# One decoder trunk, four edits: addresses of moving operands, filler pairs, embedding products, a bias table

## The chip, the cores and the metric

The kernel runs on one core of a Trainium2 chip. Its time is the device time of one execution in microseconds (us). Per core there are TensorE (PE in the rows, PEld for its weight loads), VectorE (DVE), ScalarE (ACT), GpSimd (POOL) and SyncE (SP), which issues the DMAs. [...]

## What is computed

The reference is a two-layer decoder over 1,024 tokens of width 1,024, all in float32:

```
h = rms_norm(x, g)
layer 0:  x += rms_norm((gb * conv3(gc * u)) @ w_sc_out)            gb, gc, u = h @ w_sc_in
layer 1:  x += rms_norm(diff_attention(h, k, v, dist_bias) @ w_o)   k, v from x after layer 0
both:     x += rms_norm((silu(gate) * up) @ w_down)                 gate, up = conv3(h @ w_up), 2 x 2816
both:     x += rms_norm(sigmoid(h @ w_gate) * (p_i @ w_proj))       p_i is 1024 x 256
dist_bias = rel_bias[rel_bucket(0..1023)]                           32 buckets x 8 heads
```

conv3 is causal, three taps, per channel.

## The kernel before

**Products.** Every float32 product is made of three `fp32r` matmuls: each operand is cut into a high part (ACT copy) and a low part (DVE subtract), by `split` (L305, L306) for activations and by `wsplit` (L201, L202) or `wcut` (L207, L208) for weights, and high x high, low x high and high x low are summed in PSUM (`mm3`, L318 to L320). The weights, 128 x 128, are stationary; the activations are the moving operand, channels on the partitions and 512 tokens (a "half") or 256 along the row.

**Order.** The program is a list of steps, each with a weight tile (512 KB) that is loaded two steps ahead and cut one step ahead. After each step a few "ticks" advance background generators: `gen_post` (residual, norm, operands of the next part), `gen_up` (operands of the channel mixer). A scheduler that simulates the engines then orders the instructions of each engine by readiness and by the place at which they were written, so an instruction can be issued well before its step.

**Stages.** (1) `sc_mix(0)`, `sc_mix(1)`: for each half 24 steps (moving tiles `hy`), then 8 output steps over the products `z` (moving tiles `s` of the scope `sc`). (2) `ffn(0)`: first `proj_ahead`, the embedding products `p @ w_proj` of both halves (4 steps, 96 matmuls) whose results go to DRAM (`pscr`); then the channel mixer up, NF = 22 pairs of a gate and an up tile. The first NS = 5 pairs are computed for half 0 alone in the plain way (`std_step`, 2 x 48 matmuls of 256 columns, L787); the other 17 for both halves at once by a Winograd scheme with 7 instead of 8 products (`pair_step(f, True)`, 84 matmuls of 512 columns, L809 to L811); the NS first ones are then made up for half 1 (`pair_step(f, False)`, 84 matmuls of 256). The Winograd steps need the sums T1 to T4 of the operands of both halves, which `gen_up` makes on ACT and DVE (L592, L614 to L617, L306); the plain ones need those of half 0 only. (3) `setup_attn` (L1157 to L1183): lambda, and the bias table, by three matmuls with a one-hot matrix (L1176; each float32 one is recorded as two), stores to `gscr` and eight DMAs that spread it over 128 rows of `grep`. Its small tiles come from tag `c2`, 3 buffers, that the convolutions use too. (4) `down`: 44 steps; `jit` loads the mixer's result from `hscr` and cuts it (L924 to L926). (5) `ple(0, half)`: 8 gate steps for each half; `load_pj` reads the embedding products back from `pscr`. (6) attention of layer 1, with its K, Q and V products (`pd`, L318 to L320 and L1114) between the heads' small matmuls. (7) `mix1_out`, `ffn(1)` with its own `proj_ahead`, `down`, `ple(1, half)`, and the end.

**Where tiles lie.** A pool lays its tags out in the order of their first use, each tile rounded up to 32 bytes; the pools follow each other: `cpool` (constants), `wpool` (weights), `work`, `hypool` (40 tiles `hy` of 2,048 bytes), and then the scopes `sc`, `up`, `pq`, `att`, which take turns on the rest. `cpool` begins at a multiple of 64 bytes and holds `cst` (1,572 bytes), `ident` (512), `halo` (416), `gsub` and `neg_lam` (4 each). From these sizes all `hy` tiles and, in `up`, `pq` and `att`, all moving tiles begin at a multiple of 64 bytes, and the weight tiles `wh`, `wl` at 32 past one. In `sc` the tag `u` has three tiles of (512 + 2) x 4 = 2,056 bytes, 2,080 each when rounded up; 3 x 2,080 is 32 past a multiple of 64, so the 24 tiles `s` behind them, which hold `z`, begin at 32 past 64.

Of the kernel before, what the change touches and what calls it, by code (L numbers as in the profile page):

```python
# [15 lines left out]
D = 1024  # L16
S = 1024
HT = 512
ND = 8
NF = 22  # L20
NH = 8
# [17 lines left out]
LAG_A = 2  # L39
LAG_B = 2  # L40
TS = 20
NS = 5
PF = 8
QT = 256
END_P = ((0, 1, 2, 3), (0, 1, 2, 3))
# [18 lines left out]
def _program(tc, nc, a, ctx):  # L64
# [12 lines left out]
    def nm(s):  # L77
        uid[0] += 1
        return f"{s}_{uid[0]}"
# [54 lines left out]
    def grab(dt=F32):  # L134
        al = hy if hy.room(1) else scopes["up"][2]
        return own(al, al(dt))

    def drop(t):
        owner.pop(id(t))[0].free(1)


    cst = cpool.tile([P, C_ALL], F32, tag="cst", name="cst")
    nc.sync.dma_start(out=cst, in_=a["cvec"])
    ident = cpool.tile([P, P], F32, tag="ident", name="ident")
    make_identity(nc, ident)
    halo = cpool.tile([P, 52, 2], F32, tag="halo", name="halo")
    gsub = cpool.tile([P, 1], F32, tag="gsub", name="gsub")
    nc.vector.tensor_scalar(gsub, cst[:, C_SUB:C_SUB + 1], 1.0 - LAM0, None, ALU.mult)
# [75 lines left out]
    def step(fn, w=None, pre=None, need=(), ticks=2, g=None, makes=None):  # L224
        sink[-1].append(dict(fn=fn, w=w, pre=pre, need=need, ticks=ticks, g=g, makes=makes))

    def collect(f, *args):
        sink.append([])
        f(*args)
        return sink.pop()  # L230
# [402 lines left out]
    def drop_ops():  # L633
        for name in ("B11", "B21", "B22", "T1", "T2", "T3", "T4"):
            for hi, lo in ops[name]:
                drop(hi)
                drop(lo)
        ops.clear()
# [9 lines left out]
        ys.append(y)  # L648

    def su():  # L650
        return cur[0].tile([P, HT + 2], F32, tag="u", name=nm("u"), bufs=3)

    def sc_():
        if "up" in scopes:
# [1 line left out]
        return cur[0].tile([P, HT], F32, tag="c", name=nm("c"), bufs=3)  # L656

    def u2():
        return scopes["up"][1].tile([P, 2, HT + 2], F32, tag="u2", name=nm("u2"), bufs=2)

    def c2(dt=F32):
        return scopes["up"][1].tile([P, 2, HT], dt, tag="c2", name=nm("c2"), bufs=3)
# [105 lines left out]
    def ffn(L, filler):  # L768
# [3 lines left out]
        def std_step(f, up, hold):  # L772

            def fn(w):
                n = f + NF * up
                p_ = ps()
                for tb in range(2):
                    o = p_[:, tb * QT:(tb + 1) * QT]
                    for k in range(ND):
                        if k >= 4:  # L780
                            hi, lo = (t[:, 0:QT] for t in ops["B22" if tb else "B21"][k - 4])
                        elif tb:
                            hi, lo = ops["F"][k][:, 0:QT], ops["F"][k][:, QT:]
                        else:
                            hi, lo = (t[:, 0:QT] for t in ops["B11"][k])
                        for i, (x, y) in enumerate(((w[0], hi), (w[1], hi), (w[0], lo))):
                            last_mm[0] = nc.tensor.matmul(o, x[:, k128(k)], y, skip_group_check=True,  # L787
                                                          start=(tb == 0 and k == 0 and i == 0),
                                                          stop=(k == ND - 1 and i == 2)).ins
                u = u2()[:, 0, :]  # L790
                nc.scalar.copy(out=u[:, 2:], in_=p_)
                c = conv(p_, u, 8 + n, 0, C_FF + 3 * (44 * L + n), p_)
                if not up:
                    nc.scalar.activation(c, c, AF.Silu)
                    hold["g"] = c
                else:
                    nc.vector.tensor_tensor(c, hold["g"], c, ALU.mult)
                    store(0, f, c)
                    if f == NS - 1:
                        for t in ops["F"]:  # L800
                            drop(t)
            return fn
# [19 lines left out]
        def pair_step(f, both):  # L822

            def fn(w):
                cols = slice(0, HT) if both else slice(QT, HT)
                m = HT if both else QT
                hs = slice(0, 2) if both else slice(1, 2)
                n1, n2 = f, f + NF
                wc1, wc2 = (C_FF + 3 * (44 * L + n) for n in (n1, n2))

                def v(t):
                    return t[:, 0:m].rearrange("p (h c) -> p h c", c=QT)

                def keep(p_):
                    t = wk("rb", bufs=3)
                    nc.scalar.copy(out=t[:, 0:m], in_=p_[:, 0:m])
                    return t

                a_, b_, c_ = ps(), ps(), ps()
                u, g = u2(), u2()  # L840
                product(a_[:, 0:m], w["A11"], "B11", cols, True, True)
                p1 = keep(a_)
                product(b_[:, 0:m], w["A12"], "B21", cols, True, True)
                nc.vector.tensor_tensor(g[:, hs, 2:2 + QT], v(b_), v(p1), ALU.add)
                product(a_[:, 0:m], w["S2"], "T2", cols, False, True)
                q2 = keep(a_)
                product(c_[:, 0:m], w["S1"], "T1", cols, True, True)
                p5 = keep(c_)
                product(a_[:, 0:m], w["S3"], "T3", cols, False, True)
                nc.vector.tensor_tensor(u[:, hs, 2 + QT:], v(a_), v(p5), ALU.add)  # L850
                product(c_[:, 0:m], w["S4"], "B22", cols, False, True)
                nc.vector.tensor_tensor(g[:, hs, 2 + QT:], v(c_), v(q2), ALU.add)
                if both:
                    cg = conv_both(g, wc1)
                else:
                    cg = conv(None, g[:, 1, :], 8 + n1, 1, wc1, g[:, 1, 2:])
                nc.scalar.activation(cg, cg, AF.Silu)
                product(a_[:, 0:m], w["A22"], "T4", cols, False, True)
                nc.scalar.copy(out=u[:, hs, 2:2 + QT], in_=v(a_))
                if both:  # L860
                    cu = conv_both(u, wc2)
                else:
                    cu = conv(None, u[:, 1, :], 8 + n2, 1, wc2, u[:, 1, 2:])
                nc.vector.tensor_tensor(cu, cg, cu, ALU.mult)
                if both:
                    for half in range(2):
                        store(half, f, cu[:, half, :])
                else:
                    store(1, f, cu)
            return fn  # L870

        def wup(n):
            return a["w_ffn_up"][L, n]

        steps.extend(filler)
        for f in range(NS):
            hold = {}
            for up in range(2):
                step(std_step(f, up, hold), wup(f + NF * up), need=[("h0", L)], ticks=4)
        for f in range(NS, NF):  # L880
            step(pair_step(f, True), (wup(f), wup(f + NF)), need=[("T", L)])
        for f in range(NS):
            step(pair_step(f, False), (wup(f), wup(f + NF)))
        step(lambda _: drop_ops(), None, ticks=0)
        if L == 0:
            step(lambda _: setup_attn(), None, ticks=0)
        order = [(half, k) for half in range(2) for g in range(2) for k in range(NF)]
        ahead = deque()
        at = [0]

        def fetch():
            while at[0] < len(order) and len(ahead) < PF:
                half, k = order[at[0]]
                at[0] += 1
                t = scopes["up"][2]()
                nc.sync.dma_start(out=t, in_=hscr[half, k])
                ahead.append(t)

        def jit():
            fetch()  # L900
            t = ahead.popleft()
            j = c2(F32R)
            split(j[:, 0, :], j[:, 1, :], t)
            scopes["up"][2].free(1)
            return j

        def down(half):
# [36 lines left out]

    def ple(L, half, targets):
        pj = []
        def load_pj(_):
            for n in range(ND):
                t = sc_alloc("pq")()()
                nc.sync.dma_start(out=t, in_=pscr[half, n])  # L950
                pj.append(t)

        step(load_pj, None, ticks=0)
        ys = []
        acc = [None]
        key = (f"ple{L}", half)
# [1 line left out]
        def gate_step(n):  # L958
            def fn(w):
# [13 lines left out]
                ys.append(y)  # L973
                if n == ND - 1:
                    free_h(key)
                    scopes["pq"][2].free(ND)
                    have[f"y_ple{L}", half] = (ys, acc[0])
                    bg.append(gen_post(half, (f"y_ple{L}", half), f"post_ple{L}", targets, last=(L == 1),
                                       spill=(L == 0), defer=(L == 0)))
# [389 lines left out]
    bg.append(gen_first(0))  # L1369
    step(lambda _: bg.append(gen_first(1)), None, need=[("mix0", 0)], ticks=0)  # L1370
    sc_mix(0)
    sc_mix(1)
    step(close_scope("sc"), None, ticks=0)
    step(open_scope("up", TS), None, ticks=0)
    for L in range(2):
        ffn(L, collect(proj_ahead, L, 0) + collect(proj_ahead, L, 1))
        step(close_scope("up"), None, ticks=0)
        step(open_scope("pq", 28), None, ticks=0)
        if L == 0:
# [105 lines left out]
```

## Time and profile before

| | us |
|---|---|
| median of the runs (2741.11, 2741.92, 4281.74) | 2741.92 |
| the profiled execution's own time | 2739.69 |
| its span, first to last instruction | 2737.9 |
| TensorE busy | 2587.8 |
| VectorE busy | 1854.8 |
| ScalarE busy | 1286.3 |
| mean granted clock of TensorE | 0.974 |

The profiled execution lies 2.2 us below the median and 1.8 us above its span. In the rows, busy time of TensorE counts a matmul to its modelled end; as matmuls overlap, the distance between two starts tells the rate. "[6.02 <-ACT wh L207]" behind an instruction is the idle time of its engine before it, and what ended it.

### The profile page before, as it was taken

To read this page: it belongs to the slowest core of one execution; us is meant where nothing else is said; L and a number is where in the kernel's file an instruction comes from. 1 tells how busy PE (TensorE), PEld (TensorE's weight loads), DVE (VectorE), ACT (ScalarE), POOL (GpSimd) and SP (SyncE) were. 2 spreads that over 40 slices of the span, in tenths; PEclk is the share of its full clock that TensorE was granted. 3 is DMA by queue.
4 is the path that set the end of the run, shared out by engine and by line. 5 is a ranking of instruction groups with operands and counts; after the bars stand their busy time and mean duration, and the time that the engine had idled before them with its cause. 6 is when DMAs were issued, how large, how long until landed. Compare 5 with 4: busy or idle time off the path is not lost.

```text
span 2737.9 us, 35057 instructions
## 1 busy us (share of the span) xinstructions
PE 2587.8 (95%) x12958; PEld 2127.0 (78%) x12958; DVE 1854.8 (68%) x3166; ACT 1286.3 (47%) x2182; POOL 109.4 (4%) x318
## 2 busy tenths in 40 slices
PE   8999998999997999996999999899799999899995
PEld 7888887888885887875788878688688888787875
DVE  7546469777786458569566665558886768647667
ACT  5233355444444445446555555446444445444542
POOL 0000002000000000000000000000000000000001
PEclk9999999999998999997999999999899999999997
DMA  5233252222225664343111111266222222656342
GB/s 179 93 100 123 92 186 97 85 77 85 77 93 195 231 213 154 123 142 120 55 47 55 47 62 47 93 223 217 77 70 85 77 85 97 238 189 207 116 169 77
DMA packets 128571, 328.39 MB, mean 120 GB/s; under 512 B 14360, under 2 KB 16704, under 8 KB 128400
## 3 DMA queue, kind: packets, MB, share of 16 engines
q1 hardware_dynamic: 128400, 326.16, 34.9%
q8 instruction: 101, 1.65, 0.3%
q14 instruction: 70, 0.57, 0.1%
HBM read 270.49 MB, written 60.33 MB: 121 GB/s over the span
## 4 chain that ended last, share of the span: by engine, by line
PE 87%; DVE 6%; ACT 3%; DMA 2%; issue 2%; DVEq 0%; SPq 0%; ACTq 0%
PE ps L809 8%; PE ps L810 8%; PE ps L811 8%; PE ps L318 8%; PE ps L319 8%; PE ps L320 8%; PE ps L926 6%; PE ps L924 6%; PE ps L925 6%; PE ps L787 4%; PE pd L1114 4%; PE qk L1221 3%; PE pd L318 2%; PE st L1262 2%; PE pd L319 2%; PE pd L320 2%
## 5 line engine op out<-in xcount | busy, mean ns | idle before, releaser
L202 DVE TENSOR_TENSOR wl<-wr,wh 128x1024 fp32r<-128x1024 f32 x228 | 278.9, 1224 | 237.9 <-ACT wh L201 189.4
L201 ACT CAST wh<-wr 128x1024 fp32r<-128x1024 f32 x228 | 239.6, 1053 | 337.9 <-PE ps L926 151.4
L809 PE MATMUL ps<-hy,wh 128*128 128x512 f32 (+1 forms) x924 | 337.8, 374 | 17.0 <-ACT hy L305 11.0
L810 PE MATMUL ps<-hy,wl 128*128 128x512 f32 (+1 forms) x924 | 344.2, 374 | 10.2 <-DVE wl L208 10.2
L924 PE MATMUL ps<-c,wh 128*128 128x512 f32 x704 | 281.8, 400 | 5.2 <-ACT c L305 5.2
L925 PE MATMUL ps<-c,wl 128*128 128x512 f32 x704 | 281.0, 399 | 0.0
L207 ACT CAST wh<-wr 128x1024 fp32r<-128x1024 f32 x132 | 138.3, 1050 | 214.4 <-PE ps L811 191.5
L926 PE MATMUL ps<-c,wh 128*128 128x512 f32 x704 | 232.1, 398 | 2.0 <-DVE c L306 2.0
L811 PE MATMUL ps<-hy,wh 128*128 128x512 f32 (+1 forms) x616 | 229.2, 373 | 4.6 <-DVE hy L306 4.6
L318 PE MATMUL ps<-hy,wh 128*128 128x512 f32 x552 | 220.4, 400 | 7.2 <-ACT hy L390 7.2
L319 PE MATMUL ps<-hy,wl 128*128 128x512 f32 x552 | 219.8, 399 | 0.0
L320 PE MATMUL ps<-hy,wh 128*128 128x512 f32 x552 | 219.2, 398 | 0.0
L809 PEld LDWEIGHTS ps<-hy,wh 128*128 128x128 f32 x924 | 173.8, 190 | 51.9 <-ACT hy L305 12.4
L810 PEld LDWEIGHTS ps<-hy,wl 128*128 128x128 f32 x924 | 175.7, 190 | 45.3 <-DVE wl L208 12.5
L208 DVE TENSOR_TENSOR wl<-wr,wh 128x1024 fp32r<-128x1024 f32 x132 | 161.0, 1223 | 22.0 <-ACT wh L207 21.7
L924 PEld LDWEIGHTS ps<-c,wh 128*128 128x128 f32 x704 | 133.8, 190 | 38.1 <-ACT c L305 5.9
L811 PE MATMUL ps<-s,wh 128*128 128x512 f32 (+1 forms) x440 | 162.1, 370 | 0.0
L926 PEld LDWEIGHTS ps<-c,wh 128*128 128x128 f32 x704 | 132.9, 189 | 35.4 <-DVE c L306 3.7
L925 PEld LDWEIGHTS ps<-c,wl 128*128 128x128 f32 x704 | 133.9, 190 | 32.1
L305 ACT CAST c<-s 128x512 fp32r<-128x512 f32 x176 | 108.6, 619 | 102.6 <-PE ps L926 94.2
L331 DVE TENSOR_TENSOR acc<-acc,sq 128x512 f32<-128x512 f32 x165 | 112.9, 688 | 60.7 <-ACT sq L330 58.2
L306 DVE TENSOR_TENSOR c<-s,c 128x512 fp32r<-128x512 f32 x176 | 120.8, 688 | 47.5 <-ACT c L305 47.5
(233 smaller groups left out, 5669.8 us busy)
## 6 DMA issues: line engine op xcount, KB each, us to landing
wr<-w_ffn_up SPq DMA_DIRECT2D x108, 512.0 KB, 3.4
s<-hscr SPq DMA_DIRECT2D x176, 256.0 KB, 3.4
wr<-w_ffn_down SPq DMA_DIRECT2D x88, 512.0 KB, 3.3
wr<-w_sc_in SPq DMA_DIRECT2D x48, 512.0 KB, 3.3
hscr<-c SPq DMA_DIRECT2D x88, 256.0 KB, 3.1
wr<-w_ple_gate SPq DMA_DIRECT2D x32, 512.0 KB, 3.3
xscr<-hy SPq DMA_DIRECT2D x40, 256.0 KB, 2.4
hy<-xscr SPq DMA_DIRECT2D x40, 256.0 KB, 5.5
```

What stands on the lines that cost most here:

```text
L201: nc.scalar.copy(out=hi[:, :n], in_=raw[:, :n])
L202: nc.vector.tensor_tensor(lo[:, :n], raw[:, :n], hi[:, :n].bitcast(F32), ALU.subtract)
L208: nc.vector.tensor_tensor(lo, src, hi.bitcast(F32), ALU.subtract)
L318: nc.tensor.matmul(out, whi[:, c], hi, start=(i == 0), stop=False)
L319: nc.tensor.matmul(out, wlo[:, c], hi, start=False, stop=False)
L320: last_mm[0] = nc.tensor.matmul(out, whi[:, c], lo, start=False, stop=(i == n - 1)).ins
L809: nc.tensor.matmul(o, hi[:, c], bh, skip_group_check=True, start=start and j == 0, stop=False)
L810: nc.tensor.matmul(o, lo[:, c], bh, skip_group_check=True, start=False, stop=False)
L811: last_mm[0] = nc.tensor.matmul(o, hi[:, c], bl, skip_group_check=True, start=False, stop=stop and j == 3).ins
L924: nc.tensor.matmul(o, hi[:, c], j[:, 0, :], start=(k == 0), stop=False)
L925: nc.tensor.matmul(o, lo[:, c], j[:, 0, :], start=False, stop=False)
L926: last_mm[0] = nc.tensor.matmul(o, hi[:, c], j[:, 1, :], start=False, stop=(k == NF - 1)).ins
```

## The change

1. Two unused tiles of 32 bytes in `cpool` (`pad0` before `ident`, `pad1` behind it) and one in `work` (`pad`); `u` and `u2` rows are 528 floats instead of 514. By the sizes above, `hy`, `ident` and the tiles `s`, `c2`, `kq`, `w5h`, `w5l` of all scopes then begin at 32 past 64, the weights stay at 32 past 64, and attention's `s` and `at`, stationary operands, go from 32 to 0.
2. NS is 8 in layer 0 and 7 in layer 1.
3. Layer 0's embedding products leave the start of `ffn(0)`: each half's two steps stand ahead of its gate steps in `ple(0, half)`, and their results stay in `pq` tiles. Layer 1 is as before.
4. `setup_attn` stands between `sc_mix(0)` and `sc_mix(1)`, with tiles `c` of `sc` (3 buffers).
5. `fetch` is called once before the last make-up step and may take `hy` tiles.

```diff
+UW = 528
-NS = 5
+NS = (8, 7)
...
+    def grab_up(dt=F32):
+        al = scopes["up"][2] if scopes["up"][2].room(1) else hy
+        return own(al, al(dt))
...
+    cpool.tile([P, 8], F32, tag="pad0", name="pad0")
+    work.tile([P, 8], F32, tag="pad", name="pad", bufs=1)
     ident = cpool.tile([P, P], F32, tag="ident", name="ident")
     make_identity(nc, ident)
+    cpool.tile([P, 8], F32, tag="pad1", name="pad1")
...
     def su():
-        return cur[0].tile([P, HT + 2], F32, tag="u", name=nm("u"), bufs=3)
+        return cur[0].tile([P, UW], F32, tag="u", name=nm("u"), bufs=3)[:, 0:HT + 2]
...
     def u2():
-        return scopes["up"][1].tile([P, 2, HT + 2], F32, tag="u2", name=nm("u2"), bufs=2)
+        return scopes["up"][1].tile([P, 2, UW], F32, tag="u2", name=nm("u2"), bufs=2)[:, :, 0:HT + 2]
...
-        for f in range(NS):
+        for f in range(NS[L]):
             hold = {}
             for up in range(2):
                 step(std_step(f, up, hold), wup(f + NF * up), need=[("h0", L)], ticks=4)
-        for f in range(NS, NF):
+        for f in range(NS[L], NF):
             step(pair_step(f, True), (wup(f), wup(f + NF)), need=[("T", L)])
-        for f in range(NS):
+        for f in range(NS[L]):
             step(pair_step(f, False), (wup(f), wup(f + NF)))
+            if f == NS[L] - 2:
+                step(lambda _: fetch(), None, ticks=0)
         step(lambda _: drop_ops(), None, ticks=0)
-        if L == 0:
-            step(lambda _: setup_attn(), None, ticks=0)
+        def fetch():
+            while at[0] < len(order) and len(ahead) < PF:
+                half, k = order[at[0]]
+                if not can(1):
+                    break
+                at[0] += 1
+                t = grab_up()
+                nc.sync.dma_start(out=t, in_=hscr[half, k])
+                ahead.append(t)
...
     def ple(L, half, targets):
         pj = []
+        pt = []
+
+        def load_p():
+            for k in range(2):
+                t = wk("hn")
+                nc.sync.dma_start(out=t, in_=a["pT"][L, half, k])
+                hi, lo = sc_alloc("pq")()(F32R), sc_alloc("pq")()(F32R)
+                split(hi, lo, t)
+                pt.append((hi, lo))
+
+        def proj_step(b):
+            def fn(w):
+                if b == 0:
+                    load_p()
+                for n in range(4):
+                    p_ = ps()
+                    mm3(p_, w[0], w[1], pt, lambda i: slice((n * 2 + i) * P, (n * 2 + i + 1) * P))
+                    t = sc_alloc("pq")()()
+                    nc.scalar.copy(out=t, in_=p_)
+                    pj.append(t)
+            return fn
...
-        step(load_pj, None, ticks=0)
+        if L == 0:
+            for b in range(2):
+                step(proj_step(b), a["w_ple_proj"][L, b])
+        else:
+            step(load_pj, None, ticks=0)
...
     sc_mix(0)
+    step(lambda _: setup_attn(), None, ticks=0)
     sc_mix(1)
...
-        ffn(L, collect(proj_ahead, L, 0) + collect(proj_ahead, L, 1))
+        ffn(L, collect(proj_ahead, 1, 0) + collect(proj_ahead, 1, 1) if L else [])
```

## Rows read from the trace of the kernel before

**Rows 1.** The page: the chain that ended last, share of the span by engine.

```profile
PE 87%; DVE 6%; ACT 3%; DMA 2%; issue 2%; DVEq 0%; SPq 0%; ACTq 0%
```

**Rows 2.** Windows: stretch, length, busy us (count) by engine, granted clock, DMA share, GB/s.

```profile
147.00:190.00 43.00, 43.00 (x191) 35.61 (x190) 17.47 (x20) 16.77 (x25) 0.18 (x1) 1.00 0.32 102
500.00:543.00 43.00, 43.00 (x186) 34.68 (x185) 34.01 (x38) 19.23 (x25) 1.23 (x9) 1.00 0.23 76
...
2420.00:2463.00 43.00, 43.00 (x185) 34.60 (x185) 20.76 (x25) 17.47 (x25) 0.00 (x0) 1.00 0.56 188
```

**Rows 3.** Timeline of TensorE: first matmul over `z` of half 0, first after the last.

```profile
146.78 0.39 PE L318 MATMUL ps<-s,wh 128*128 128x512 f32 x1
...
190.33 0.40 PE L318 MATMUL ps<-hy,wh 128*128 128x512 f32 x1
```

**Rows 4.** Timeline of TensorE, 256 columns: two places in a plain step, two in V.

```profile
430.02 0.28 PE L787 MATMUL ps<-s,wl 128*128 128x256 f32 x1
...
431.20 0.40 PE L787 MATMUL ps<-s,wh 128*128 128x256 f32 x2
...
1438.18 0.28 PE L1114 MATMUL pd<-wl,hy 128*128 128x256 f32 x1
...
1440.82 0.40 PE L1114 MATMUL pd<-wh,hy 128*128 128x256 f32 x2
```

**Rows 5.** Timeline of TensorE between up and down, layer 0, then layer 1.

```profile
871.80 3.57 PE L1176 MATMUL st<-c,rs_b 32*8 32x512 f32 x4 [13.62 <-DMA c<-onehot]
877.56 0.58 PE L1176 MATMUL st<-c,rs_b 32*8 32x128 f32 x2 [2.19 <-DMA c<-onehot]
879.00 0.80 PE L924 MATMUL ps<-c,wh 128*128 128x512 f32 x1 [0.86 <-ACT c L305]
...
2354.54 0.79 PE L924 MATMUL ps<-c,wh 128*128 128x512 f32 x1 [4.38 <-ACT c L305]
```

**Rows 6.** DMA issues from 880 to 915 us: count, size, median time to landing.

```profile
grep<-gscr SPq DMA_DIRECT2D x8, 576.0 KB, 8.7
```

**Rows 7.** Windows, as rows 2: start of `ffn(0)`, gates of half 1, entrance to attention, `ffn(1)`.

```profile
371.50:472.00 100.50, 88.33 (x618) 81.38 (x618) 90.69 (x169) 63.83 (x111) 14.52 (x21) 0.96 0.43 145
1182.00:1230.00 48.00, 47.63 (x203) 38.45 (x204) 34.34 (x73) 21.83 (x41) 0.00 (x0) 0.95 0.39 135
1230.00:1313.00 83.00, 49.68 (x248) 40.57 (x247) 75.01 (x190) 48.42 (x110) 0.00 (x0) 0.80 0.33 114
1941.00:1966.00 25.00, 9.71 (x29) 6.72 (x30) 25.00 (x51) 11.11 (x24) 0.28 (x2) 0.71 0.13 46
```

**Rows 8.** Timeline of TensorE: waits in `ffn(0)`, and ahead of the gates of half 1.

```profile
372.40 0.50 PE L318 MATMUL ps<-c,wh 128*128 128x512 f32 x1 [1.68 <-ACT c L305]
...
466.15 1.22 PE L809 MATMUL ps<-hy,wh 128*128 128x512 f32 x2 [6.02 <-ACT wh L207]
472.22 0.79 PE L810 MATMUL ps<-hy,wl 128*128 128x512 f32 x1 [4.85 <-DVE wl L208]
...
1182.37 0.80 PE L318 MATMUL ps<-s,wh 128*128 128x512 f32 x1 [4.75 <-ACT s L390]
```

**Rows 9.** Timeline of TensorE: the same point of two make-up steps, two steps apart.

```profile
826.87 0.38 PE L810 MATMUL ps<-hy,wl 128*128 128x256 f32 x1 [0.76 <-DVE wl L208]
...
849.16 0.38 PE L810 MATMUL ps<-hy,wl 128*128 128x256 f32 x1 [0.73 <-DVE wl L208]
```

**Rows 10.** Groups of VectorE from 371.5 to 472 us: count, busy us, mean ns.

```profile
L202 DVE TENSOR_TENSOR wl<-wr,wh 128x1024 fp32r<-128x1024 f32 x12 | 14.6, 1219 | 1.9 <-ACT wh L201 1.9
L592 DVE SCALAR_TENSOR_TENSOR s<-hy,cst,st 128x256 f32<-128x256 f32 x16 | 6.8, 474 | 0.0
L673 DVE SCALAR_TENSOR_TENSOR c<-u,cst,c 128x512 f32<-128x512 f32 x9 | 6.7, 748 | 5.4 <-ACT c L672 5.4
L797 DVE TENSOR_TENSOR c<-c,c 128x512 f32<-128x512 f32 x4 | 2.7, 684 | 0.0
L306 DVE TENSOR_TENSOR c<-hn,c 128x512 fp32r<-128x512 f32 x4 | 2.7, 688 | 0.4 <-ACT c L305 0.3
```

More of the change, by code (lines that the diff above doesn't have):

```diff
@@ L798, in fn @@
                     store(0, f, c)
-                    if f == NS - 1:
+                    if f == NS[L] - 1:
                         for t in ops["F"]:
@@ L849, in fn @@
                 product(a_[:, 0:m], w["S3"], "T3", cols, False, True)
-                nc.vector.tensor_tensor(u[:, hs, 2 + QT:], v(a_), v(p5), ALU.add)
+                nc.vector.tensor_tensor(u[:, hs, 2 + QT:2 + 2 * QT], v(a_), v(p5), ALU.add)
                 product(c_[:, 0:m], w["S4"], "B22", cols, False, True)
-                nc.vector.tensor_tensor(g[:, hs, 2 + QT:], v(c_), v(q2), ALU.add)
+                nc.vector.tensor_tensor(g[:, hs, 2 + QT:2 + 2 * QT], v(c_), v(q2), ALU.add)
                 if both:
@@ L889, in ffn @@
         at = [0]
[L891 to L897, printed above, removed]
         def jit():
@@ L903, in jit @@
             split(j[:, 0, :], j[:, 1, :], t)
-            scopes["up"][2].free(1)
+            drop(t)
             return j
@@ L975, in fn @@
                     free_h(key)
-                    scopes["pq"][2].free(ND)
+                    scopes["pq"][2].free(ND + (4 if L == 0 else 0))
                     have[f"y_ple{L}", half] = (ys, acc[0])
```

## The prediction

> **What bounds the kernel now.** I read the page first, then windows stage by stage, then the timeline of TensorE where it idles. TensorE is busy 2587.8 of 2737.9 us (table above), and the chain that ended last runs over it for 87% [rows 1]. So the bound is TensorE's rate, and at a few seams what TensorE waits for.
>
> The rate differs between stages at the same full clock. In 43 us, 191 matmuls of 512 columns start over `z`, and 186 or 185 over other tiles, one or two of each count lying across an edge [rows 2]. The output steps of half 0 are 8 x 24 = 192 matmuls, and their starts take 190.33 - 146.78 = 43.55 us [rows 3], 226.8 ns each. 43 us at that rate are 189.6, so 1.4 of a count are strays; the others' mean, 185.5 - 1.4 = 184.1, gives 233.6 ns, the lower count 234.2, and I take 234. DVE and ACT are no reason: at 0.79 DVE (34.01 of 43) and at 0.48 (20.76 of 43) the count is the same, while `z` ran at 0.41 [rows 2]. What sets `z` apart is its address, 32 past 64 bytes instead of 0.
>
> The seams are these. TensorE idles 6.02 and 4.85 us in `ffn(0)` before the Winograd steps, and 15.3 of 25 us in `ffn(1)` [rows 7, 8]; DVE is busy 90.69 of 100.5 us in the one and all 25 in the other. Between up and down of layer 0 it idles 13.62 + 2.19 + 0.86 us round the bias table, where layer 1 idles 4.38 [rows 5]. Before the gates of half 1 it idles 4.75 us [rows 8], and from 1230 to 1313 us it works 49.68 of 83, with DVE at 75.01 [rows 7].
>
> **The change part by part**, against the profiled execution's own 2739.7 us.
>
> *Addresses.* Matmuls of 512 columns by the loops: first stage 1,152 + 384 (`z`), embeddings 192, pairs 34 x 84 = 2,856, down 2,112, gates 696, attention's output 384, K and Q 768; 8,544 in all. With 15 pairs made the plain way instead of 10 the pairs are 29 x 84 = 2,436; without `z`, which stays at 32, 7,740 move. Outside attention 6,972 x 7.2 ns (234 - 226.8) = 50.2 us. In attention K and Q give 768 x 7.2 = 5.5 us if their steps still bound it; heads' matmuls of 512 columns over `kq` lie between other sizes. I take 5 for all. Together -55. Ends: -44, if a fifth is lost to waits that then show, and -57. The wider rows cost DVE and ACT nothing that a row shows: the lengths of the operations stay.
>
> Matmuls of 256 columns have no row with both operands at 32. In the plain steps (moving at 0) 10 starts take 431.20 - 430.02 us, 118 ns each; in V (moving weights at 32, stationary at 0) 22 take 1440.82 - 1438.18, 120 ns [rows 4]. By V nothing is gained; by half of 7.2 ns, 1,440 plain and 768 V matmuls would give 8 us. V is the nearest row: I take 0, with ends of +4 and -8.
>
> *Bias table.* The idle times round it in layer 0 add up to 16.67 us and its matmuls to 3.57 + 0.58 = 4.15; layer 1's seam shows what is left, 4.38 us, since there the cuts wait for the last convolution to leave `c2`, which the early `fetch` doesn't alter (0 for that edit; ends 0 and -3 a layer) [rows 5]. So 16.67 + 4.15 - 4.38 = 16.4 us go. In the first stage the three products come back, at most at 4.15 us, half at the full clock; I take 3. Its DMA chain (lambda, one-hot, stores, eight spreads) runs under the output steps of half 0, 43.55 us of TensorE work with DVE at 17.47 of 43 [rows 2, 3]; it queues on SP before the weight loads of half 1. The eight spreads landed 8.7 us after issue [rows 6], against weights two steps (11 us) ahead: covered, 0; if the cover fails, up to 8. Its tiles take the three `c` buffers, which the output steps don't use. Net -13.5, ends -5 and -16.
>
> *Embedding products.* 96 matmuls change place. In half 1 their 48 (48 x 0.227 = 10.9 us) fill the 4.75 us ahead of the gates [rows 8], and the low clock behind it (0.95 over 48 us, 2.4 us) [rows 7]: -7.1. Ahead of half 0 nothing idled; the cut of `p` may be late as it was at 372.40, 1.68 us [rows 8]: +1. The stores and loads of `pscr` go, which had cover. At the entrance to attention DVE is the bound: 33.3 us idle on TensorE [rows 7]. Two blocks of 10.9 us ahead of it ask DVE for 4 x (1.22 + 0.69) = 7.6 us [rows 10], so DVE gains 14 us on its backlog; the last gate's chain to the operands of half 1 stays. Ends 0 and -14, I take -6: the chain is most of it. Together -12.
>
> *Pairs.* A plain pair costs 96 x 0.118 = 11.33 us, its make-up step 11.15 ((849.16 - 826.87) / 2, bound by the weights' cut, not by TensorE) [rows 4, 9], and the Winograd step that it replaces 84 x 0.2268 = 19.05: +3.4 us a pair, five pairs +17. In return TensorE has work while the operands are made. A plain pair asks DVE for 2 x 1.22 + 4 x 0.75 + 0.68 = 6.1 us [rows 10], so it leaves DVE 5.2 us for the operands.
> Layer 1 keeps its embedding products and gets two pairs: 10.4 of the 15.3 us idle [rows 7] go; -10, ends -4 and -15.
> Layer 0 loses 96 x 0.234 = 22.5 us of products that asked DVE for 7.6, a margin of 14.9, and gets three pairs with a margin of 15.6: the wait for the operands stays, -1, ends -8 and +8. New is a wait at the start: the plain steps need half 0's operands, of which DVE makes the last four channel tiles (the 16 of L592 into `s`, 6.8 us [rows 10], and their cuts) when the scope `up` is open, until now under the embedding products. Some of it can start earlier, on tiles that lie where the first stage's small ones were. +4, ends 0 and +10.
>
> Sum: -55 - 13.5 - 12 + 17 - 10 - 1 + 4 = -70.5, or 2669.2 for the profiled execution; 2.2 us above it, as the median was, 2671.
>
> [...]
>
> **The rivals.**
> *The address does nothing* (`z` is fast by something of its steps). For it: only one stage shows 227. Against it: equal counts at two loads of DVE [rows 2]. Then the 55 us stay, and the pairs cost 5 x 0.6 us less: 2671 + 55 - 3 = 2723. Chance 0.08.
> *DVE stays the bound at the seams*: the operands in `ffn(1)` come as late as before (0 instead of -10), the start of `ffn(0)` costs 10, the entrance to attention gives 0. For it: DVE full in [rows 7]. Then 2671 + 10 + 6 + 6 = 2693. Chance 0.17.
> *More is hidden*: 256 columns gain the 8 us, and attention's entrance all 14: 2671 - 16 = 2655. For it: V's stationary tiles lie at 0, so no row has 256 columns with both at 32; against it: V's 120 ns [rows 4]. Chance 0.22.
> *32 is the slow side*: what V shows against the plain steps, 2 ns for 256 columns, holds everywhere, 4 ns for 512, and `z` is fast by something else. Place: all products; price: 7,740 x 4 ns + 1,440 x 2 = 34 us instead of -55. 2671 + 55 + 34 = 2760, slower than before. It decides from some 2 ns for 512 columns on, where it eats the remaining -15. For it: [rows 4]; against it: `z`'s 192 matmuls [rows 3] and V's other neighbours, small matmuls of the heads. Chance 0.03.
>
> **How the numbers follow.** The forecast has 0.50, with 2656 to 2686 of its own (the seams, 3 to 4 terms of about 6 us). A measurement of this kernel tells about 2% from no change, that is 2687. Below it lie the forecast, "more is hidden" and a quarter of "DVE stays the bound": 0.50 + 0.22 + 0.04 = 0.76. Above 2797 lies next to nothing: 0.02, the tail of the last rival and of a queue that I have not seen. The rest, 0.22, is within 2%. The range from 2643 to 2698 holds all but the first and last rival and the tails.
>
> **What would show it.** Right: starts of 512-column matmuls 227 ns apart in pairs, down and gates; no idle time round L1176; no wait ahead of the gates of half 1; `ffn(1)` idle under 8 us before its first Winograd step. Wrong steps: 234 ns anywhere (addresses); a wait for weights near 190 us (the spreads' DMAs); over 10 us idle at the first plain step of layer 0; make-up steps longer than 11.2 us. The prediction as a whole is wrong if the 7.2 ns fail, or if the waits for the operands grow by more than 20 us in all.

## The result, and the profile after

The changed kernel takes 2704.01 us (median of four runs, 2702.35 to 2705.30) against 2743.47 for the kernel before: 0.9859 of its time, interval 0.9839 to 0.9878, some 38 us or 1.4% less. (One run of the kernel before, at 4281.74 us, counts in its median and not in the ratio; without it the median is 2741.92.) The forecast was 2671, its range 2643 to 2698: the result lies outside. The profiled execution took 2703.73 us, its span is 2701.9 against 2737.9, 36.0 less, and the mean granted clock, a share of the full one, 0.98 against 0.974.

The page of the changed kernel, the chain that ended last, by engine:

```profile
PE 85%; DVE 9%; ACT 2%; DMA 2%; issue 2%; DVEq 0%; SPq 0%; ACTq 0%
```

TensorE is the bound as before [rows 1]. In the changed kernel's lines `mm3` is L327 to L329, the plain step L796, the Winograd step L818 to L820, down L935 to L937, V L1151, the bias table's product L1213, the weights' cuts L210 and L211 or L216 and L217, the activations' L314 and L315.

Windows of the changed kernel (stretch, length, busy us and count of PE, PEld, DVE, ACT, POOL, granted clock, DMA share, GB/s): output steps over `z`, pairs, start of `ffn(0)`, gates with their products, entrance to attention.

```profile
147.00:190.00 43.00, 43.00 (x184) 33.93 (x183) 17.53 (x23) 17.07 (x27) 0.18 (x1) 1.00 0.26 88
500.00:543.00 43.00, 43.00 (x186) 34.73 (x185) 30.48 (x33) 17.60 (x22) 2.64 (x9) 1.00 0.24 84
...
374.64:490.00 115.36, 99.28 (x815) 96.08 (x814) 101.96 (x185) 64.95 (x109) 27.70 (x31) 0.96 0.33 107
...
1104.99:1219.71 114.72, 114.72 (x505) 92.38 (x505) 91.41 (x164) 66.40 (x112) 0.00 (x0) 1.00 0.36 122
1219.71:1283.87 64.16, 47.23 (x249) 38.90 (x248) 55.23 (x153) 38.32 (x93) 0.00 (x0) 0.86 0.33 115
```

The first two rows answer to [rows 2]. The pairs still start 186 matmuls of 512 columns in 43 us, as before, and `z` has lost its lead: 184 instead of 191. So the rate that the forecast built on did not come, and the one stage that had it lost it. The exception is small: in the Winograd steps the 348 matmuls whose weights are the tiles `w5h` and `w5l` start 228.4 ns apart on average, those with `wh` and `wl` around them 233.3. The gates of layer 0 now run without a gap at the full clock. The same two stretches of the kernel before, which held 96 products fewer:

```profile
1131.84:1243.48 111.64, 94.83 (x408) 75.89 (x407) 78.84 (x149) 51.34 (x89) 0.00 (x0) 0.93 0.46 159
1243.48:1315.04 71.56, 50.05 (x248) 41.14 (x249) 62.63 (x163) 42.02 (x98) 0.00 (x0) 0.81 0.23 81
```

Timeline of TensorE in the changed kernel (start, us, engine, line, operands, idle before and what ended it): `z` of half 0 with the table's products, the starts of `ffn(0)`, two make-up steps, the seam to down, gates and entrance, and `ffn(1)`.

```profile
146.50 0.39 PE L327 MATMUL ps<-s,wh 128*128 128x512 f32 x1
...
163.33 1.02 PE L1213 MATMUL st<-c,rs_b 32*8 32x512 f32 x2
...
192.37 1.02 PE L1213 MATMUL st<-c,rs_b 32*8 32x512 f32 x2
...
193.32 0.50 PE L327 MATMUL ps<-hy,wh 128*128 128x512 f32 x1
...
377.52 0.39 PE L796 MATMUL ps<-hy,wh 128*128 128x256 f32 x1 [1.31 <-ACT wh L210]
378.60 0.39 PE L796 MATMUL ps<-hy,wh 128*128 128x256 f32 x1 [0.68 <-ACT hy L314]
382.86 0.39 PE L796 MATMUL ps<-hy,wh 128*128 128x256 f32 x1 [2.15 <-ACT hy L314]
...
482.27 1.22 PE L818 MATMUL ps<-hy,wh 128*128 128x512 f32 x2 [7.07 <-ACT wh L216]
488.35 0.80 PE L819 MATMUL ps<-hy,wl 128*128 128x512 f32 x1 [4.86 <-DVE wl L217]
...
805.18 0.38 PE L819 MATMUL ps<-hy,wl 128*128 128x256 f32 x1 [0.76 <-DVE wl L217]
816.19 0.38 PE L819 MATMUL ps<-hy,wl 128*128 128x256 f32 x1 [0.76 <-DVE wl L217]
...
851.46 0.50 PE L935 MATMUL ps<-c,wh 128*128 128x512 f32 x1 [4.38 <-ACT c L314]
...
1104.99 0.50 PE L327 MATMUL ps<-s,wh 128*128 128x512 f32 x1 [2.02 <-ACT s L314]
...
1260.47 0.79 PE L327 MATMUL pd<-hy,wh 128*128 128x512 f32 x1 [6.53 <-ACT hy L1159]
1280.81 0.45 PE L379 MATMUL st<-ident,rs_k 128*128 128x128 f32 x1 [6.09 <-DVE rs_k L359]
...
1942.87 1.22 PE L818 MATMUL ps<-hy,wh 128*128 128x512 f32 x2 [6.57 <-ACT wh L216]
1947.13 0.79 PE L819 MATMUL ps<-hy,wl 128*128 128x512 f32 x1 [3.05 <-DVE wl L217]
```

The waits round the bias table [rows 5] are gone, and what stands at that seam is layer 1's 4.38 us. In `ffn(1)` 6.57 + 3.05 = 9.6 us are idle ahead of the Winograd steps, where 15.3 were [rows 7]. In layer 0 those waits are about what they were, 7.07 and 4.86 for 6.02 and 4.85 [rows 8], with 4.1 us new at the first plain steps.

From the first matmul of each stage in both timelines comes where the 36.0 us went. The scheduler mixes the first make-up steps with the last Winograd steps; their stage is counted from the point where matmuls of 256 columns alone are left. All lengths are in us:

| stage | before | after | difference |
|---|---|---|---|
| span's start to `ffn(0)` | 372.40 | 374.64 | +2.2 |
| `ffn(0)` up to the make-up steps | 433.10 | 386.03 | -47.1 |
| make-up steps and seam to down | 73.50 | 90.79 | +17.3 |
| down 0 | 252.84 | 253.53 | +0.7 |
| gates 0, entrance to attention | 183.20 | 178.88 | -4.3 |
| attention | 474.13 | 472.85 | -1.3 |
| mix-out and products of layer 1 | 93.07 | 95.72 | +2.7 |
| `ffn(1)` up to the make-up steps | 415.58 | 386.74 | -28.8 |
| make-up steps and seam to down | 56.72 | 79.85 | +23.1 |
| down 1 | 252.41 | 252.00 | -0.4 |
| the rest | 130.95 | 130.87 | -0.1 |

### The profile page after: what moved, and what is told of

Same layout as the page of the kernel before. It is cut to its first block, busy times and chain, and to the rows that moved or that the text cites. A ratio compares the mean times of both kernels' runs of the same rounds, so it can differ in the third digit from the quotient of the medians.

```text
span 2701.9 us, 36095 instructions
## 1 busy us (share of the span) xinstructions
PE 2581.3 (96%) x13438; PEld 2137.5 (79%) x13438; DVE 1866.8 (69%) x3201; ACT 1296.4 (48%) x2216; POOL 158.1 (6%) x328
## 4 chain that ended last, share of the span: by engine, by line
PE 85%; DVE 9%; ACT 2%; DMA 2%; issue 2%; DVEq 0%; SPq 0%; ACTq 0%
PE ps L327 8%; PE ps L328 8%; PE ps L329 8%; PE ps L819 7%; PE ps L820 7%; PE ps L818 7%; PE ps L937 6%; PE ps L936 6%; PE ps L935 6%; PE ps L796 4%; PE pd L1151 4%; PE qk L1258 3%; PE st L1299 2%; PE pd L327 2%; PE pd L328 2%; PE pd L329 2%
## 5 line engine op out<-in xcount | busy, mean ns | idle before, releaser
L211 DVE TENSOR_TENSOR wl<-wr,wh 128x1024 fp32r<-128x1024 f32 x238 | 290.9, 1223 | 231.5 <-ACT wh L210 179.4
L210 ACT CAST wh<-wr 128x1024 fp32r<-128x1024 f32 x238 | 249.9, 1051 | 349.9 <-PE ps L937 148.4
L819 PE MATMUL ps<-hy,wl 128*128 128x512 f32 (+1 forms) x924 | 329.8, 359 | 16.8 <-DVE wl L217 16.8
L818 PE MATMUL ps<-hy,wh 128*128 128x512 f32 (+1 forms) x924 | 316.5, 359 | 13.6 <-ACT wh L216 13.6
L935 PE MATMUL ps<-c,wh 128*128 128x512 f32 x704 | 279.6, 397 | 8.8 <-ACT c L314 8.8
L216 ACT CAST wh<-wr 128x1024 fp32r<-128x1024 f32 x132 | 137.8, 1047 | 209.5 <-PE ps L820 154.2
L937 PE MATMUL ps<-c,wh 128*128 128x512 f32 x704 | 231.2, 397 | 2.0 <-DVE c L315 2.0
L327 PE MATMUL ps<-hy,wh 128*128 128x512 f32 x552 | 218.3, 397 | 8.3 <-ACT hy L399 8.3
L820 PE MATMUL ps<-hy,wh 128*128 128x512 f32 (+1 forms) x616 | 219.2, 357 | 0.0
L329 PE MATMUL ps<-hy,wh 128*128 128x512 f32 x552 | 217.8, 396 | 0.0
L818 PEld LDWEIGHTS ps<-hy,wh 128*128 128x128 f32 x924 | 171.8, 190 | 44.4 <-ACT wh L216 16.6
L217 DVE TENSOR_TENSOR wl<-wr,wh 128x1024 fp32r<-128x1024 f32 x132 | 160.8, 1221 | 17.1 <-ACT wh L216 16.9
L935 PEld LDWEIGHTS ps<-c,wh 128*128 128x128 f32 x704 | 132.8, 189 | 41.1 <-ACT c L314 9.3
L937 PEld LDWEIGHTS ps<-c,wh 128*128 128x128 f32 x704 | 132.7, 189 | 35.9 <-DVE c L315 3.8
L314 ACT CAST c<-s 128x512 fp32r<-128x512 f32 x175 | 108.1, 619 | 104.4 <-PE ps L937 93.6
L820 PE MATMUL ps<-s,wh 128*128 128x512 f32 (+1 forms) x440 | 154.6, 356 | 0.0
L315 DVE TENSOR_TENSOR c<-s,c 128x512 fp32r<-128x512 f32 x175 | 120.2, 688 | 47.8 <-ACT c L314 47.8
```

What stands on the lines that cost most here:

```text
L210: nc.scalar.copy(out=hi[:, :n], in_=raw[:, :n])
L211: nc.vector.tensor_tensor(lo[:, :n], raw[:, :n], hi[:, :n].bitcast(F32), ALU.subtract)
L217: nc.vector.tensor_tensor(lo, src, hi.bitcast(F32), ALU.subtract)
L327: nc.tensor.matmul(out, whi[:, c], hi, start=(i == 0), stop=False)
L329: last_mm[0] = nc.tensor.matmul(out, whi[:, c], lo, start=False, stop=(i == n - 1)).ins
L818: nc.tensor.matmul(o, hi[:, c], bh, skip_group_check=True, start=start and j == 0, stop=False)
```

## The experiments

The first question was the address. Two theories stood after the result. *Place*: the moving operand's start counts (32 past 64 bytes against 0). *Distance*: what counts is where the weights begin less where the moving tile begins, modulo some power of two; `z` differed from nearly all other tiles in that as well. Worked out from the sizes and the order of the tags, the weights began at 160 modulo 512 bytes and `hy` at 64 in the kernel before, distance 96, and `z` at 160, distance 0. The change moved the weights by the two pads of `cpool`, 64 bytes, and `hy` by all three, 96: distance 64. `z` went to distance 128. The four runs e1 to e4 share a chip and 2742.05 us for the kernel before.

**e1_pads_out: the addresses of before.**

```diff
-UW = 528
+UW = 514
-    cpool.tile([P, 8], F32, tag="pad0", name="pad0")
-    work.tile([P, 8], F32, tag="pad", name="pad", bufs=1)
-    cpool.tile([P, 8], F32, tag="pad1", name="pad1")
```

> The changed kernel without the three pad tiles and with u and u2 rows of 514 floats again, so hy and the other moving tiles are back at 0 past 64. Two theories. Place: the start of the moving tile past 64 bytes sets the rate. Distance: the offset of the stationary tile (which is loaded while the matmul runs) from the moving one, modulo 256 bytes, sets it; it was 96 in the kernel before, 0 for z there, 64 in the changed kernel. Both expect 512 columns back at 234 ns and 256 columns at 118, z at 227, and 8 + 6 + 2 us more than the changed kernel: about 2720. What the two pads are worth on their own is the point.

Measured: 2714.07 us, 0.9901 (0.9884 to 0.9917). The address edit as it was made is worth 10 us, where the forecast had 55. (Down of layer 0 is not back where it was: its tiles are at distance 32 in e1, since without the embedding products the tags of the scope `up` come in another order.) Windows of e1, TensorE alone: pairs, then plain steps.

```profile
500.00:543.00 43.00, 43.00 (x186) 1.00 0.22 74
400.00:443.00 43.00, 43.00 (x369) 1.00 0.54 172
```

**e2_64_more, e3_192_more, e4_all_32_more: other distances, other places.** From the changed kernel, one pad each:

```diff
# e2: moving tiles 64 bytes further, distance 0
-    work.tile([P, 8], F32, tag="pad", name="pad", bufs=1)
+    work.tile([P, 24], F32, tag="pad", name="pad", bufs=1)
# e3: 192 bytes further, distance 128
+    work.tile([P, 56], F32, tag="pad", name="pad", bufs=1)
# e4: weights and moving tiles both 32 bytes further, distance 64 as in the changed kernel
-    cpool.tile([P, 8], F32, tag="pad1", name="pad1")
+    cpool.tile([P, 16], F32, tag="pad1", name="pad1")
```

> The changed kernel with 64 bytes more ahead of the work tiles: all moving tiles stay at 32 past 64, the stationary ones stay where they are, the distance goes from 64 to 0 (256 for down's tiles). Place expects no change: 233 ns, 2704 us. Distance expects 227 ns for some 7,700 matmuls of 512 columns, 6 ns less each, and 256 columns back at about 118: -46 + 8, about 2666 us.

> As the run with 64 bytes more, but 192 more: moving tiles at 32 past 64, distance 384 modulo 512, which is 128 modulo 256 (192 for z). Place: 2704. Distance: unknown between the rates seen, 227 to 234 for 512 columns; if the period is 128 and not 256, as for a distance of 0: 2666. It maps the distance.

> The changed kernel with 32 bytes more ahead of the weight tiles, which moves stationary and moving tiles alike: all begin at 0 past 64, the distance is 64 as in the changed kernel. Place expects the rates of the kernel before, 234 and 118 ns, about 2720 us. Distance expects no change: 233 and 114 ns, 2704 us.

Measured: e2 2667.77 us, 0.9727 (0.9713 to 0.9742); e3 2707.05, 0.9869 (0.9854 to 0.9883); e4 2704.23, 0.9861 (0.9846 to 0.9875). The same two windows of e2:

```profile
500.00:543.00 43.00, 43.00 (x191) 1.00 0.25 85
400.00:443.00 43.00, 43.00 (x362) 1.00 0.50 160
```

Of e3, the pairs alone:

```profile
500.00:543.00 43.00, 43.00 (x187) 1.00 0.22 76
```

Of e4, and then the plain steps of the changed kernel:

```profile
500.00:543.00 43.00, 43.00 (x186) 1.00 0.22 76
400.00:443.00 43.00, 43.00 (x379) 1.00 0.53 171
...
400.00:443.00 43.00, 43.00 (x379) 1.00 0.54 173
```

e4 has its moving tiles at 0 past 64 bytes, where Place loses all that the pads brought; it keeps the changed kernel's time and its two counts (186 and 379) instead. Place falls. e2 keeps the moving tiles at 32 past 64, where they were in the changed kernel, and alters the distance alone: 36 us come, and 191 starts in 43 us, the rate that `z` once had. e3 shows that 128 bytes are not 0 (187 starts where e2 has 191), so the period is longer than 128. A place counted modulo more than 64 falls too: `hy` of the changed kernel begins at 64 + 96 = 160, where `z` began in the kernel before, and is slow there. The pad of e2 moves operands of DVE and ACT as well, but the matmuls explain its gain: by the table below, 7,392 x 6.2 ns less 1,440 plain ones x 5.9 and 768 of V x 2.9 is 35.1 us of 36.2.

**e8_96_more and e9_160_more: two distances more,** with pads of 32 and 48 floats in `work`, distances 224 and 160.

> The changed kernel with 96 bytes more ahead of the work tiles: distance 224 modulo 256, moving tiles at 0 past 64. Distance: between its neighbours 192 (228.9 and 116.8 ns for 512 and 256 columns) and 0 (227.0 and 119.7), so about 228 and 118 and 2675 us. Place: the rates of the kernel before, 234 and 118, and 2714.

> The changed kernel with 160 bytes more: distance 160 modulo 256, moving tiles at 0 past 64. Distance: between its neighbours 128 (232.5 ns) and 192 (228.9), so about 231 ns and 2695 us. Place: 234 and 2714. It closes the map of the distance in steps of 32.

Measured: e8 2706.51 us, 0.9871 (0.9856 to 0.9886); e9, a single run, 2710.56. Both theories' numbers were missed. For Distance I had interpolated between distances already measured, and the time doesn't interpolate. Place, for which e8 had 2714, had fallen already. Windows of e8, then of e9:

```profile
500.00:543.00 43.00, 43.00 (x186) 1.00 0.21 74
400.00:443.00 43.00, 43.00 (x371) 1.00 0.55 173
```

```profile
500.00:543.00 43.00, 43.00 (x187) 1.00 0.22 76
400.00:443.00 43.00, 43.00 (x361) 1.00 0.54 171
```

From the traces of all these runs, the mean distance in time between the starts of neighbouring matmuls of one size, those behind a wait left out (ns), by the distance in bytes modulo 256, which is worked out from the tile sizes as above, since the traces hold no addresses:

| bytes | 512 columns | 256 columns | seen in |
|---|---|---|---|
| 0 | 227.1 | 119.8 | e2, e10, e11 |
| 32 | 233.3 | 118.2 | down 0 of e1; V of e8 |
| 64 | 233.3 | 113.9 | after; e4 |
| 96 | 234.2 | 117.8 | before; e1 |
| 128 | 232.5 | 118.7 | e3 |
| 160 | 233.4 | 120.0 | e9 |
| 192 | 228.9 | 116.9 | `z` of e3; V of after |
| 224 | 233.3 | 116.8 | e8 |

A period of 256 fits all of it: in e2 distance 0 gives 227.1 and 256 gives 226.8; in the changed kernel 64 and 320 give 233.3 both. Its `w5` weights lie at 256, and theirs are the 228.4 ns above. So 64 bytes, where the change landed, are slow for 512 columns and the fastest seen for 256.

**e11_before_at_0: the kernel before, with distance 0 and nothing else.** `z` keeps its distance of 0 by a wider `u`.

```diff
+    work.tile([P, 24], F32, tag="pad", name="pad", bufs=1)
-        return cur[0].tile([P, HT + 2], F32, tag="u", name=nm("u"), bufs=3)
+        return cur[0].tile([P, 640], F32, tag="u", name=nm("u"), bufs=3)[:, 0:HT + 2]
-        return scopes["up"][1].tile([P, 2, HT + 2], F32, tag="u2", name=nm("u2"), bufs=2)
+        return scopes["up"][1].tile([P, 2, 528], F32, tag="u2", name=nm("u2"), bufs=2)[:, :, 0:HT + 2]
```

> The kernel before with nothing changed but the addresses: 96 bytes ahead of its work tiles and u and u2 rows of 640 and 528 floats, which puts every moving tile at a distance of 0 from the weights. Distance: 8,160 matmuls of 512 columns at 227 instead of 234 ns, -57, and 960 of 256 at 119.7 instead of 118, +2: 2687 us. Rival: part of it comes back as waits at the seams, as the forecast's lower end had it: 2698.

Measured: 2693.41 us against 2742.01, 0.9818 (0.9802 to 0.9834): 48.6 us from the distance alone, between the two expectations. It is more than the whole change of this case brought. Its windows:

```profile
500.00:543.00 43.00, 43.00 (x192) 1.00 0.26 87
400.00:443.00 43.00, 43.00 (x361) 1.00 0.41 133
```

**The other parts, each undone alone** from the changed kernel; e5 to e7 share a chip and 2741.95 us for the kernel before.

**e5_bias_back**

```diff
+        if L == 0:
+            step(lambda _: setup_attn(), None, ticks=0)
...
     sc_mix(0)
-    step(lambda _: setup_attn(), None, ticks=0)
```

> The changed kernel with the bias table made after layer 0's channel mixer again, as before. If the move is worth what the seam showed, 16.4 us less some 3 us of matmuls and waits in the first stage, this takes 13 us more: 2717. Rival: the seam's time is given back elsewhere (the DMAs of the spread, the first stage), and it stays at 2704.

Measured: 2715.93 us, 0.9907 (0.9892 to 0.9922), 12 more than the changed kernel. Timeline of e5 at the seam:

```profile
858.44 3.58 PE L1215 MATMUL st<-c,rs_b 32*8 32x512 f32 x4 [13.31 <-DMA c<-onehot]
864.20 0.58 PE L1215 MATMUL st<-c,rs_b 32*8 32x128 f32 x2 [2.18 <-DMA c<-onehot]
865.64 0.80 PE L937 MATMUL ps<-c,wh 128*128 128x512 f32 x1 [0.86 <-ACT c L314]
```

The waits of [rows 5] are back nearly to the number. Make-up steps and seam take 107.14 us against 90.79, the forecast's 16.4; the first stage is 2.1 us shorter without the products. In the changed kernel's trace `z` of half 0 takes 193.32 - 146.50 = 46.82 us, 3.3 more than before [rows 3]: 192 starts at 232.4 ns are 44.6, so 2.2 are the table's products and 1.1 are what `z` lost by its new distance.

**e6_products_back**: layer 0's embedding products at the start of `ffn(0)` again, through `pscr`, with 8 and 7 pairs kept.

```diff
-        if L == 0:
-            for b in range(2):
-                step(proj_step(b), a["w_ple_proj"][L, b])
-        else:
-            step(load_pj, None, ticks=0)
+        step(load_pj, None, ticks=0)
...
-        ffn(L, collect(proj_ahead, 1, 0) + collect(proj_ahead, 1, 1) if L else [])
+        ffn(L, collect(proj_ahead, L, 0) + collect(proj_ahead, L, 1))
```

> The changed kernel with layer 0's embedding products at the start of its channel mixer again, stored and read back as before; 8 and 7 plain pairs stay. The trace of the changed kernel shows the stretch from the first gate to the attention's steady part 4 us shorter than before although it holds 22 us more of products, which makes the move worth 26 us there; in the channel mixer the products come back (22.5) but cover some 14 us of its waits. So 4 + 22.5 - 14 = 12 us more: 2716. Rival, the forecast's own sizes: 12 us lost at the gates, 15 won at the waits, so 2701.

Measured: 2713.88 us, 0.9899 (0.9883 to 0.9916), 10 more. Timeline of e6, first at the start of `ffn(0)`, then at the gates and the entrance:

```profile
377.44 0.51 PE L327 MATMUL ps<-c,wh 128*128 128x512 f32 x1 [1.68 <-ACT c L314]
398.90 0.50 PE L327 MATMUL ps<-c,wh 128*128 128x512 f32 x1 [1.55 <-ACT u L1096]
...
1164.99 0.80 PE L327 MATMUL ps<-s,wh 128*128 128x512 f32 x1 [4.75 <-ACT s L399]
```

With the products back and eight pairs the waits ahead of the Winograd steps are gone, and only the two rows of 1.68 and 1.55 are left in the first half of `ffn(0)`. Up to the make-up steps it takes 391.2 us against 386.0, though it holds 96 x 0.2333 = 22.4 us more work. Gates and entrance take 181.8 against 178.9, though they hold 22.4 less: the 4.75 us of [rows 8] and the idle entrance are back. So the products cover waits in either place: the move gains at the gates some 25 us of idle time and low clock, and gives back some 17 in `ffn(0)`. The rival with the forecast's own sizes, 2701, is out.

**e7_five_pairs**: `NS = (5, 5)` in place of `(8, 7)`.

> The changed kernel with 5 plain pairs in both layers again. If plain pairs are cover for VectorE's work on the operands, at 2.3 us a pair, the waits before the first Winograd step grow by 15 us in layer 0 and by 6 to 10 in layer 1, and 11 us of work go: 2704 + 23 - 11 = 2716. Rival: VectorE, which a plain pair loads too, sets when the operands come, the waits stay as they are, and only the work goes: 2693.

Measured: 2713.68 us, 0.9898 (0.9884 to 0.9913), 10 more, near the first expectation's 2716; the rival's 2693 is out. Timeline of e7: the start of `ffn(0)`, the Winograd steps there, and those of `ffn(1)`.

```profile
376.74 0.38 PE L796 MATMUL ps<-hy,wh 128*128 128x256 f32 x1 [1.31 <-ACT wh L210]
377.81 0.39 PE L796 MATMUL ps<-hy,wh 128*128 128x256 f32 x1 [0.69 <-ACT hy L314]
382.08 0.39 PE L796 MATMUL ps<-hy,wh 128*128 128x256 f32 x1 [2.11 <-ACT hy L314]
...
445.26 1.11 PE L379 MATMUL st<-ident,rs_r 128*128 128x128 f32 x4 [8.56 <-DVE rs_r L359]
447.38 0.80 PE L818 MATMUL ps<-hy,wh 128*128 128x512 f32 x1 [1.01 <-ACT hy L314]
452.76 0.80 PE L820 MATMUL ps<-hy,wh 128*128 128x512 f32 x1 [3.30 <-DVE hy L315]
462.91 0.50 PE L818 MATMUL ps<-hy,wh 128*128 128x512 f32 x1 [2.66 <-ACT hy L314]
467.01 0.80 PE L820 MATMUL ps<-hy,wh 128*128 128x512 f32 x1 [3.36 <-DVE hy L315]
...
1916.83 0.50 PE L818 MATMUL ps<-hy,wh 128*128 128x512 f32 x1 [2.12 <-ACT hy L314]
1922.62 0.80 PE L820 MATMUL ps<-hy,wh 128*128 128x512 f32 x1 [4.60 <-DVE hy L315]
1936.64 0.79 PE L818 MATMUL ps<-hy,wh 128*128 128x512 f32 x1 [7.50 <-ACT hy L314]
1939.57 0.80 PE L818 MATMUL ps<-hy,wh 128*128 128x512 f32 x1 [1.71 <-ACT hy L314]
```

The three pairs of layer 0 pay: without them 23.0 us are idle instead of 16.1, in eight places, and the stage with its seam is 6.8 us longer, though it has less work; the idle time grew by 7 us where 15 were expected, and the stretch's granted clock fell from 0.99 to 0.97. Layer 1's two pairs do so barely: its mixer's up stage and seam are 3.3 us longer without them, but the stage ahead, which lost 2.7 us in the table, is 3.0 shorter.

**e10_64_more_10_8**: e2 with `z` at distance 0 too (`u` of 640 floats) and `NS = (10, 8)`, against the waits that e2 left.

> The changed kernel with 64 bytes more (distance 0), the first stage's u tiles 640 floats wide so that z is at 0 too, and 10 and 8 plain pairs instead of 8 and 7. z gives 384 matmuls times 6 ns, 2 us. If a plain pair still covers 5 us of wait for 3.4 us of work, three more give 5 us: 2661. Rival: VectorE stays the bound at the seam, the waits stay and the work comes on top: 2676.

Measured: 2665.88 us, 0.9723 (0.9708 to 0.9737), between the two expectations. By its interval it can't be told from e2's 0.9727. Timeline of e10 ahead of the first Winograd steps of layer 0:

```profile
494.46 0.73 PE L818 MATMUL ps<-hy,wh 128*128 128x512 f32 x2 [0.71 <-ACT wh L216]
496.78 0.50 PE L819 MATMUL ps<-hy,wl 128*128 128x512 f32 x1 [1.59 <-DVE wl L217]
```

The idle time there falls to 2.3 us, and the work of the three pairs added, 96 x 0.1198 + 11.0 - 84 x 0.2271 = 3.4 us each, about eats what is gained. e2 and e10 are 2.7 to 2.8% faster than the kernel before, and both beat the changed kernel.

## Why the prediction was wrong

**The failed step is "What sets `z` apart is its address, 32 past 64 bytes instead of 0"**, and with it the term of -55; the prediction itself had called the whole wrong if the 7.2 ns fail. The measured difference of 7.2 ns was real: e11 has it in every stage, e2 in every one but `z`, 227.1 ns against 234.2. Its cause was misread. In the trace of before `z` differed by its place and by its distance from the weights, at once, and of the other 8,160 matmuls of 512 columns 7,480 had one distance, 96. One trace couldn't tell the two apart, and I named the one that the diff speaks of. With the weights moved by 64 and the moving tiles by 96 the distance became 64, and the 512-column matmuls gained 234.2 - 233.3 = 0.9 ns instead of 7.2: 7,740 x 0.9 = 7 us, less 384 x 5.4 ns = 2 that `z` lost.

**256 columns**, taken as 0 from V, the nearest row, gained 118 to 113.9 ns in the plain steps. V was no guide, since its weights are the moving operand and its distance another. A pair now costs 96 x 0.1139 + 11.0 - 84 x 0.2333 = 2.3 us instead of 3.4, five pairs +11.5 instead of +17; on the ten old ones and on V it is some 6 us more. The end of -8 held. With the 5 us above, the edit as a whole is the 10 us of e1.

**Bias table**, -13.5: right. The seam gave the 16.4 us, the first stage cost 2.2, about the half of 4.15 that the forecast set for the full clock (granted 0.50 from 871 to 879 us of before, 1.00 from 163 to 165 us here), no weights came late behind the eight spreads (they landed 7.5 us after issue, and TensorE has no idle time from 190 to 330 us), and the early `fetch` left the 4.38 us of layer 1's seam as they were. e5 gives 12.

**Embedding products**, -12: too small. The stretch from the first gate to the end of the entrance is 4.3 us shorter and holds 22.4 us more work, so 26.7 went there. The waits ahead of the gates of half 1 went as said. The term failed at the entrance, for which I took -6 of 0 to -14 on the ground that "the last gate's chain to the operands of half 1 stays". In the two windows idle time fell from 16.8 + 21.5 to 0 + 16.9 us, and the 2.0 at 1104.99 are new: -19.4 in all. The rest is the clock, 0.93 to 1.00 and 0.81 to 0.86, of which I had counted the gates of half 1 alone. DVE worked off in the longer first stretch what had made the entrance wait: it is busy 91.41 us there instead of 78.84, and 55.23 instead of 62.63 in the second.

**The waits.** Layer 0: +3 by the forecast (-1 and +4), and 16.1 us idle where 6.02 + 4.85 [rows 8] and two smaller ones, 1.68 and 0.61, stood: +3. The first plain steps do wait for half 0's operands, 4.1 us with the first cut. Layer 1: -5.7 against -10, near the end of -4, and 2.7 us came back in the stage ahead of it, which was not forecast; 2.1 of them are a wait at layer 1's embedding products. A make-up step takes 816.19 - 805.18 = 11.0 us, as before bound by the weights' cut.

**The sum.** Terms as measured: addresses -11, bias -14, embedding -27, pairs +11.5, waits +3 - 6 + 3 = -40; the span shows -36, so some 4 us stand in no term, 1.2 of them a later first matmul. Of the 35 us by which the forecast was too low, the addresses alone are over 40 and the waits 7; the embedding products gave 15 back and the pairs 5. The rival "the address does nothing" was nearest in mechanism and 19 us too high, because it took over the small embedding term. "DVE stays the bound", 2693, had a nearer time by the wrong mechanism: the waits went about as forecast. The range failed since it left that first rival out at 0.08. A cause told from a single stage of one trace deserved less.

Undone one by one, the four parts are worth 10 (addresses), 12 (bias), 10 (products) and 10 us (pairs), 42 in all against the 38 measured. By this sum they depend little on each other, but products and pairs cover the same wait in `ffn(0)`, and no run undid two at once. The early `fetch` was not undone alone.

**What stays open.** Which part of the hardware makes the distance count, whether it is the weights in use or those loaded beside them, and why 64 bytes suit 256 columns (113.9 ns) and 0 suits 512 (227.1). `wh` and `wl` lie alike, so their distances are the same. The `w5` weights lie elsewhere, but the 27 places per run where one kind follows the other don't agree. In the changed kernel it is 225.7 ns with 0 in use and 64 next, 232.1 the other way round; in e9 it is 236.6 with 0 in use and 160 next, and 230.0 the other way round. Neighbours seem to count too: the 85 matmuls of the kernel before that had distance 0 beside ones at 64 started some 233 ns apart, in e11, where all are at 0, 227. Giving each size its own distance was not tried.

## What to carry to other kernels

A TensorE rate that differs between stages at the full clock is worth chasing through the addresses of both operands, not of one; here, bringing weights and moving tiles to the same place modulo 256 bytes gave 36 us on top of the changed kernel, and 49 us in the kernel before, where the whole change gave 38. Before a cause read from one odd stage is priced over the whole kernel, move both suspects together, and one of them alone: that takes two runs. Work that is moved as a filler is worth the idle time and the low clock at its new place, less the same at its old one (here, by e6, some 25 us less some 17), and the second is as easily forgotten as the clock.

## What the runs showed of the hardware

Not expected: in these runs the time between the starts of neighbouring matmuls went with the distance of their two operands' addresses modulo 256 bytes, from 227.1 (0 bytes) to 234.2 ns (96) for 512 columns, and from 113.9 (64) to 120.0 ns (160) for 256, with the order of the distances different for the two sizes. The place of the moving operand past 64 bytes, 0 in e4 and 32 in the changed kernel, changed nothing where the distance stayed at 64: 2704.23 against 2704.01 us.
